# Two-layer block on one core: 169 low parts of weights made by ScalarE and an adding DMA instead of GpSimd

## The chip, the cores and the metric

The kernel runs on one core of one Trainium2 chip. A core has a matrix engine (PE), whose weight loads are listed as PEld, a vector engine (DVE), a scalar engine (ACT), a general engine (POOL, also GpSimd) and an engine that issues DMAs (SP). Each has its own instruction queue and works through it in order; they meet through semaphores. All DMAs share 16 DMA engines. Time is device microseconds of one execution, and the time of a kernel is the median of its runs.

## What is computed

The reference runs 512 tokens of width 1024 through two blocks. The first has two layers: a pooling and latent attention layer, then a differential attention layer, each followed by a gated feed-forward net. The second mixes three kinds of attention or recurrence and then routes each token to 128 of 16384 experts. What the change touches are the weights of the differential attention, of the second feed-forward net, of the mixing layer and of the router's queries:

```python
qkv = hn @ w_qkv                                   # differential attention
...
h = h + swiglu(rmsnorm(h, ffn_norm_g[layer]), ffn_w_gate[layer], ffn_w_up[layer], ffn_w_down[layer])
...
proj = h @ w_in[l]                                 # second block: 13 x 256 columns
...
x = x + mixed @ w_out[l]
...
q = (x_blk @ w_query).reshape(b, t, PEER_HEADS, 2, HALF_KEY)
scores = jnp.einsum('bthcd,hcnd->bthcn', q, sub_keys).astype(jnp.float32)
top_s, top_i = lax.top_k(scores, PEER_TOPK)
```

## The kernel before

Every large product is made of three products of a shorter float format: a weight w is split into a high part `whi` (w rounded) and a low part `wlo` = w - `whi`, the tokens likewise, and PE adds high by high, high by low and low by high (L266 to L268; L283 to L285 where tokens are rows). The function `load_w` brings a block of weights in two halves of up to 128x1024 float32 (512 KB). For a half SP issues a DMA into `raw` (L253), ACT copies `raw` into `whi` (L228), and DVE or POOL subtracts: `wlo` = `raw` - `whi` (L229, in `split`). `raw`, `whi` and `wlo` have three buffers each (`RB, WB = 3, 3`), shared by all weights in turn, so that a half can be begun only when PE has done with the half three before it. With 256 columns of tokens a half feeds 24 matrix products.

Who subtracts is set by `low(n)`: of the two halves of a block the first n go to POOL and the others to DVE. It is 2 in the differential attention (`LO_Q`), in the stage of memory and projections (`LO_Y`) and in the mixing and first routing stages (`LO_M`), 1 from the end of the first routing through the second half's projections (`LO_Z`) and in the last stages (`LO_P`), and 0 in the feed-forward nets ahead of the second block.

The stages follow each other in time roughly so, in us: differential attention 590 to 880; feed-forward of the first 256 tokens to 1070; memory and projections of half A 1075 to 1200; mixing of half A to 1322, its output, norm and first query blocks to 1422, the first routing to 1640; projections of half B to 1700, its mixing and output to 1850; then the expert stages to the end. The feed-forward of the other 256 tokens (`ffn_b`) is dealt out among the stages from 1075 to 1640 by `alongside`. Routing takes, for 8 heads and 2 tiles of tokens, the 16 largest of 128 scores twice and of their 256 sums once, all on DVE in some forty short instructions for each (L1465 to L1498).

A scheduler lays out each engine's queue from the program's order and priorities; the order is fixed when the kernel is built. In the expert stages POOL also issues gathers of 128 rows of 4 KB (L1503).

## Time and profile before

| | us |
|---|---|
| median of 3 runs | 3133.07 (3132.15 to 3140.36) |
| the profiled execution | 3134.13 |
| its span, first to last instruction | 3132.4 |
| PE busy | 2938.3 |
| DVE busy | 2207.6 |
| ACT busy | 1372.6 |
| POOL busy | 1147.2, of it subtractions of weights (L229, 241 of them) 589.8 |

Busy time is when an engine executes; waits and the issue of DMAs on SP are not in it. PE's clock has two levels, 1.2 and 2.4 GHz; the column "PEclk" or "clock" gives the granted share of the higher one. A wait is listed with the instruction that released it. The page cuts the span in 40 slices of 78.3 us; the views used below cut it at the stages' bounds.

### The profile page before, as it was taken

What the parts mean: (1) busy time and instruction counts of PE and PEld (TensorE: products, weight loads), DVE (VectorE), ACT (ScalarE), POOL (GpSimd) and SP (SyncE); (2) the same over time, 40 slices, a digit from 0 to 9 for tenths busy, and PEclk for the clock granted to TensorE, in tenths of its full rate; (3) what the DMA queues carried; (4) which work ended last, traced back from release to release, by engine and by line L of the source; (5) the groups of instructions that cost most, each with busy time, mean ns of one, the idle gap of its engine ahead of it and who ended that gap; (6) DMA issues with size and microseconds to landing.
All of it is one profiled execution on the core that took longest, in us unless ns stands there. A gap on an engine that the chain in (4) does not pass through costs nothing.

```text
span 3132.4 us, 44864 instructions
## 1 busy us (share of the span) xinstructions
PE 2938.3 (94%) x16770; PEld 2551.2 (81%) x16770; DVE 2207.6 (70%) x4148; ACT 1372.6 (44%) x2347; POOL 1147.2 (37%) x723
## 2 busy tenths in 40 slices
PE   8999999999989889998779989889999999999999
PEld 6468888867689888888769588888999998777787
DVE  6755434477766747658996569999787758888753
ACT  4443222466554545453244543336666653333333
POOL 3110000343320376466554235555554535445200
PEclk9999999999999989999889989999999999999999
DMA  3022232311145533234334038777788779999964
GB/s 132 25 67 101 88 101 88 107 54 48 35 158 194 175 132 125 87 132 142 118 112 151 1 121 281 254 274 256 275 316 305 283 286 383 382 380 370 338 229 151
DMA packets 195883, 568.30 MB, mean 181 GB/s; under 512 B 16944, under 2 KB 68528, under 8 KB 194000
## 3 DMA queue, kind: packets, MB, share of 16 engines
q1 hardware_dynamic: 157664, 427.61, 39.4%
q0 software_dynamic: 37712, 137.71, 11.9%
q8 instruction: 132, 2.16, 0.3%
q14 instruction: 87, 0.71, 0.1%
q10 hardware_dynamic: 288, 0.11, 0.0%
HBM read 512.93 MB, written 52.43 MB: 180 GB/s over the span
## 4 chain that ended last, share of the span: by engine, by line
PE 71%; DVE 21%; DMA 3%; issue 2%; ACT 2%; POOL 0%; DVEq 0%; SPq 0%; ACTq 0%; POOLq 0%
PE ps L266 15%; PE ps L267 15%; PE ps L268 15%; PE ps L1669 4%; PE ps L1670 4%; PE ps L1668 4%; PE ps L1550 2%; DVE u L1517 2%; DVE wlo L229 2%; PE ps L482 2%; DMA raw<-in_peer_v_dram 1%; PE ps L475 1%; DVE oh L1490 1%; PE ps L283 1%; PE ps L285 1%
## 5 line engine op out<-in xcount | busy, mean ns | idle before, releaser
L229 POOL TENSOR_TENSOR wlo<-raw,whi 128x1024 fp32r<-128x1024 f32 (+2 forms) x241 | 589.8, 2455 | 634.8 <-ACT whi L228 585.9
L228 ACT ACTIVATE whi<-raw 128x1024 fp32r<-128x1024 f32 (+2 forms) x518 | 516.2, 999 | 648.6 <-PE ps L267 391.8
L229 DVE TENSOR_TENSOR wlo<-raw,whi 128x1024 fp32r<-128x1024 f32 (+3 forms) x277 | 334.0, 1207 | 215.3 <-ACT whi L228 214.6
L268 PE MATMUL ps<-yh,wlo 128*128 128x384 f32 (+1 forms) x1152 | 387.5, 337 | 27.7 <-DVE wlo L229 27.6
L266 PE MATMUL ps<-yh,whi 128*128 128x384 f32 (+1 forms) x1152 | 389.9, 339 | 0.0
L267 PE MATMUL ps<-yl,whi 128*128 128x384 f32 (+1 forms) x1152 | 385.1, 334 | 0.0
L1669 PE MATMUL ps<-vl,gh 128*128 128x512 f32 x768 | 301.1, 392 | 4.2 <-DVE vl L229 4.1
L1670 PE MATMUL ps<-vh,gl 128*128 128x512 f32 x768 | 299.9, 391 | 0.0
L266 PE MATMUL ps<-XH,whi 128*128 128x512 f32 (+1 forms) x680 | 273.2, 406 | 8.7 <-ACT whi L228 8.7
L1503 POOL DMA_INDIRECT u<-in_peer_v_dram,ix x128 | 197.5, 1543 | 197.8 <-DVE h L1582 182.5
L267 PE MATMUL ps<-XL,whi 128*128 128x512 f32 (+1 forms) x680 | 267.7, 396 | 0.0
L268 PE MATMUL ps<-XH,wlo 128*128 128x512 f32 (+1 forms) x680 | 263.1, 395 | 1.3 <-DVE wlo L229 1.3
L1668 PE MATMUL ps<-vh,gh 128*128 128x512 f32 x768 | 239.8, 392 | 9.2 <-ACT vh L228 9.2
L268 PEld LDWEIGHTS ps<-yh,wlo 128*128 128x128 f32 x1152 | 220.4, 191 | 32.4 <-DVE wlo L229 32.4
L228 ACT ACTIVATE vh<-raw 128x1024 fp32r<-128x1024 f32 x128 | 133.5, 1056 | 253.9 <-DMA raw<-in_peer_v_dram 183.4
L266 PE MATMUL ps<-fx,whi 128*128 128x256 f32 x704 | 202.6, 292 | 26.0 <-ACT whi L228 21.4
L1517 DVE SCALAR_TENSOR_TENSOR u<-u,h 128x1024 f32<-128x1024 f32 x127 | 203.1, 1604 | 32.4 <-DMA u<-in_peer_u_dram,ix 32.2
L266 PEld LDWEIGHTS ps<-yh,whi 128*128 128x128 f32 x1152 | 220.9, 192 | 0.0
L267 PEld LDWEIGHTS ps<-yl,whi 128*128 128x128 f32 x1152 | 220.5, 191 | 0.0
L366 POOL TENSOR_TENSOR sqa<-sqa,sq 128x512 f32<-128x512 f32 (+1 forms) x28 | 42.1, 1505 | 450.5 <-ACT sq L364 449.6
L229 DVE TENSOR_TENSOR vl<-raw,vh 128x1024 fp32r<-128x1024 f32 x128 | 155.5, 1221 | 65.7 <-ACT vh L228 65.0
L267 PE MATMUL ps<-fx,whi 128*128 128x256 f32 x704 | 199.6, 287 | 0.9 <-DVE fx L351 0.9
(427 smaller groups left out, 7244.4 us busy)
## 6 DMA issues: line engine op xcount, KB each, us to landing
raw<-in_uT_dram SPq DMA_DIRECT2D x128, 512.0 KB
raw<-in_peer_v_dram SPq DMA_DIRECT2D x128, 512.0 KB
raw<-in_w_gate_dram SPq DMA_DIRECT2D x66, 512.0 KB
raw<-in_w_up_dram SPq DMA_DIRECT2D x66, 512.0 KB
raw<-in_w_in_dram SPq DMA_DIRECT2D x52, 512.0 KB
Sd<-s SPq DMA_DIRECT2D x32, 768.0 KB
Gd<-st SPq DMA_DIRECT2D x12, 2048.0 KB
gt<-Gd SPq DMA_DIRECT2D x32, 768.0 KB
```

Source lines behind the costliest of these rows:

```text
L228: SC.activation(hi, src, AF.Copy)
L229: eng.tensor_sub(lo, src, hi.bitcast(F))
L266: PE.matmul(out, wh, xh, start=first, stop=False)
L267: PE.matmul(out, wh, xl, start=False, stop=False)
L268: PE.matmul(out, wl, xh, start=False, stop=last)
L482: PE.matmul(po[hd], vtile(hd, j), t[hd, j], start=j == 0, stop=j == nk - 1)
L1503: i = GP.indirect_dma_start(out=u, out_offset=None, in_=A[table], in_offset=bass.IndirectOffsetOnAxis(ap=self.idx[t, hd][:, j:j + 1], axis=0))
L1517: V.scalar_tensor_tensor(u, u, 1.0, self.h2[t], op0=OP.mult, op1=OP.mult, accum_out=self.sd[t][:, hd, j:j + 1])
L1550: PE.matmul(p[:, n * 128:(n + 1) * 128], q[:, n], e[:, n], start=True, stop=True)
L1668: PE.matmul(p, gh[:, e, ts], h[:, cs], start=False, stop=False, skip_group_check=True)
L1669: PE.matmul(p, gh[:, e, ts], l[:, cs], start=False, stop=False, skip_group_check=True)
L1670: PE.matmul(p, gl[:, e, ts], h[:, cs], start=False, stop=end, skip_group_check=True)
```

## The change

A third value, `ADDED`, can stand where an engine stood. Such a half is loaded and copied to `whi` as before; then ACT also writes `wlo` = -`whi`, and POOL issues a DMA that reads the weights from DRAM once more and adds them into `wlo`. `raw` is no longer needed once `whi` is written. `low` is given `ADDED` for the differential attention, the projections, the mixing with the first routing, and the stage after it; the last stages keep POOL's subtraction.

```diff
-        def low(n):
-
-            LO[:] = [GP] * n + [V] * (2 - n)
+        ADDED = object()
+
+        def low(n, other=GP):
+
+            LO[:] = [other] * n + [V] * (2 - n)
...
-                split(hi, lo, raw, eng[i])
+                if eng[i] is ADDED:
+                    SC.activation(hi, raw, AF.Copy)
+                    SC.activation(lo, hi.bitcast(F), AF.Copy, scale=-1.0)
+                    GP.dma_start(lo, ap[:, a * w:b * w], accum_op=OP.add)
+                else:
+                    split(hi, lo, raw, eng[i])
...
-            low(LO_Q)
+            low(LO_Q, ADDED)
...
-        low(LO_Y)
+        low(LO_Y, ADDED)
         alongside((chain(memory(), projections(HA)), 24), (ffn_b, F_1))
         open_mix()
-        low(LO_M)
+        low(LO_M, ADDED)
...
-        low(LO_Z)
+        low(LO_Z, ADDED)
```

Of POOL's 241 subtractions of weights 72 stay; 169 become additions by DMA: 22 of `w_qkv`, 12 of `w_dout`, 4 of `w_mem`, 39 of `w_in`, 12 of `w_out`, 64 of the feed-forward net and 16 of `w_query`. ACT has 169 instructions more. Line numbers behind L262 grow by 7 (L266 becomes L273).

On ACT, in the projections of half A, before (`pj` and `hgv` are results of the projections, `sq` a gate):

```order
L228 ACTIVATE whi_9978<-raw_9976 128x1024
L1113 ACTIVATE hgv_9325<-ps_9918,rt_6972 128x256
L1113 ACTIVATE hgv_9325<-ps_9944,rt_6972 128x256
L228 ACTIVATE whi_10036<-raw_10034 128x1024
L228 ACTIVATE whi_10042<-raw_10040 128x1024
L1135 ACTIVATE sq_10516<-pj_9333 128x256
L228 ACTIVATE whi_10100<-raw_10098 128x1024
```

and the same blocks now:

```order
L259 ACTIVATE whi_10027<-raw_10025 128x1024
L260 ACTIVATE wlo_10028<-whi_10027 128x1024
L1120 ACTIVATE hgv_9359<-ps_9966,rt_7006 128x256
L1120 ACTIVATE hgv_9359<-ps_9992,rt_7006 128x256
L259 ACTIVATE whi_10086<-raw_10084 128x1024
L260 ACTIVATE wlo_10087<-whi_10086 128x1024
L259 ACTIVATE whi_10093<-raw_10091 128x1024
L260 ACTIVATE wlo_10094<-whi_10093 128x1024
L1142 ACTIVATE sq_10580<-pj_9367 128x256
L259 ACTIVATE whi_10152<-raw_10150 128x1024
```

Each copy is followed by the negated copy of the same half, and the other work has kept its place.

On POOL, in the first routing, before (the weights of `w_query` and `ffn_b` in turn):

```order
L229 TENSOR_TENSOR wlo_13767<-raw_13764,whi_13766 128x1024
L229 TENSOR_TENSOR wlo_13773<-raw_13770,whi_13772 128x1024
L229 TENSOR_TENSOR wlo_13855<-raw_13852,whi_13854 128x1024
L229 TENSOR_TENSOR wlo_13861<-raw_13858,whi_13860 128x1024
L229 TENSOR_TENSOR wlo_13987<-raw_13984,whi_13986 128x1024
```

and now:

```order
L261 DMA wlo_13667<-in_w_query_dram 128x1024
L261 DMA wlo_13674<-in_w_query_dram 128x1024
L261 DMA wlo_13757<-in_w_down11_dram 128x1024
L261 DMA wlo_13764<-in_w_down11_dram 128x1024
L261 DMA wlo_13891<-in_w_query_dram 128x1024
```

One DMA issue stands where one subtraction stood, and nothing else is between them in either.

On PE, in the projections of half A, where the second half of a block begins (`wlo_10043`, then `wlo_10028`), before:

```order
L266 MATMUL ps_10072<-xh_9293,whi_10042 128x256
L267 MATMUL ps_10072<-xl_9294,whi_10042 128x256
L266 MATMUL ps_10110<-xh_9293,whi_10100 128x256
L267 MATMUL ps_10110<-xl_9294,whi_10100 128x256
L266 MATMUL ps_10136<-xh_9293,whi_10100 128x256
L268 MATMUL ps_10046<-xh_9293,wlo_10043 128x256
```

and now:

```order
L273 MATMUL ps_10058<-xh_9327,whi_10027 128x256
L274 MATMUL ps_10058<-xl_9328,whi_10027 128x256
L273 MATMUL ps_10098<-xh_9327,whi_10086 128x256
L274 MATMUL ps_10098<-xl_9328,whi_10086 128x256
L273 MATMUL ps_10124<-xh_9327,whi_10086 128x256
L274 MATMUL ps_10124<-xl_9328,whi_10086 128x256
L275 MATMUL ps_10032<-xh_9327,wlo_10028 128x256
```

One product with a high part more runs ahead of the first with the low part (six instead of five); the order is otherwise as it was.

## Rows read from the trace of the kernel before

**Rows 1.** the page: the span, and busy time of each engine.

```profile
span 3132.4 us, 44864 instructions
PE 2938.3 (94%) x16770; PEld 2551.2 (81%) x16770; DVE 2207.6 (70%) x4148; ACT 1372.6 (44%) x2347; POOL 1147.2 (37%) x723
```

**Rows 2.** busy time by stage: from:to, length, PE, PEld, DVE, ACT, POOL, clock, DMA.

```profile
590.00:880.00 290.00, 284.84 (x1387) 211.03 (x1386) 202.78 (x482) 159.79 (x304) 115.17 (x74) 1.00 0.19 61
1116.00:1200.00 84.00, 79.44 (x660) 79.06 (x659) 31.88 (x70) 38.48 (x48) 63.71 (x28) 0.96 0.47 162
1200.00:1322.00 122.00, 109.20 (x751) 95.19 (x750) 94.57 (x237) 59.23 (x105) 60.72 (x50) 0.93 0.25 88
1322.00:1422.00 100.00, 92.67 (x747) 88.62 (x747) 56.05 (x131) 51.26 (x86) 62.62 (x27) 0.95 0.40 135
1422.00:1575.00 153.00, 116.16 (x899) 112.92 (x897) 150.71 (x505) 47.19 (x74) 82.56 (x35) 0.90 0.37 124
1575.00:1640.00 65.00, 48.71 (x297) 44.83 (x298) 62.31 (x171) 27.09 (x48) 35.18 (x34) 0.80 0.34 110
1640.00:1700.00 60.00, 60.00 (x518) 60.00 (x517) 29.05 (x49) 31.00 (x41) 27.57 (x11) 1.00 0.54 185
```

**Rows 3.** three of these stages, line 229 alone: DVE, then POOL.

```profile
1116.00:1200.00 84.00, 0.00 (x0) 63.67 (x27) 0.96 0.47 162
...
1322.00:1422.00 100.00, 14.91 (x21) 62.37 (x26) 0.95 0.40 135
1422.00:1575.00 153.00, 3.67 (x4) 82.56 (x35) 0.90 0.37 124
```

**Rows 4.** ACT in order of time, 1141 to 1151: start, length, idle's releaser.

```profile
1141.96 1.06 ACT L228 ACTIVATE whi<-raw 128x1024 fp32r<-128x1024 f32 x1 [1.53 <-PE ps L267]
...
1150.58 1.06 ACT L228 ACTIVATE whi<-raw 128x1024 fp32r<-128x1024 f32 x1 [1.24 <-PE ps L267]
```

**Rows 5.** a 512 KB transfer that POOL issued, and the wait for it.

```profile
L1007 POOL DMA_DIRECT2D mraw<-in_masks_dram x1: 536/536/536, 868.5 to 868.5; - x1
...
  DMA mraw<-in_masks_dram: 4.3, 1
```

**Rows 6.** POOL's DMA queue; its gathers of 512 KB: last, median us to landing.

```profile
q0 software_dynamic: 37712, 137.71, 11.9%
...
u<-in_peer_v_dram,ix POOLq DMA_INDIRECT x128, 7.8
u<-in_peer_u_dram,ix POOLq DMA_INDIRECT x127, 6.3
...
q<-in_peer_u_dram,ix POOLq DMA_INDIRECT x1, 4.6
```

**Rows 7.** groups of DVE, 1422 to 1575: count, busy us, mean ns.

```profile
L1488 DVE CAST af<-ai 128x16 f32<-128x16 int32 x24 | 20.1, 869 | 0.0
L1477 DVE TENSOR_TENSOR cand<-ts 128x256 f32<-128x256 f32 x13 | 13.9, 1071 | 0.0
L1485 DVE TENSOR_SCALAR ai<-bp 128x16 int32<-128x16 int32 x24 | 11.3, 508 | 0.0
...
L1492 DVE TENSOR_TENSOR oh<-oh,tf 128x256 f32<-128x256 f32 x23 | 9.7, 440 | 0.0
...
L1475 DVE CAST tf<-ti 128x32 f32<-128x32 uint32 x13 | 5.5, 423 | 0.0
```

**Rows 8.** groups of DVE and of POOL, 1880 to 2050.

```profile
L1488 DVE CAST af<-ai 128x16 f32<-128x16 int32 x20 | 2.9, 221 | 0.0
...
L1503 POOL DMA_INDIRECT u<-in_peer_u_dram,ix x40 | 50.2, 1254 | 24.7 <-DVE u L1517 5.7 <-DVE sc L1467 3.9 <-DVE ti L1466 3.6
```

**Rows 9.** DVE, then POOL, in order of time around 1494.

```profile
1494.03 2.23 DVE L1488 CAST af<-ai 128x16 f32<-128x16 int32 x2
...
1493.75 2.40 POOL L229 TENSOR_TENSOR wlo<-raw,whi 128x1024 fp32r<-128x1024 f32 x1 [0.98 <-ACT whi L228]
```

**Rows 10.** waits, 1422 to 1575: who, for whom, us in total, times, longest.

```profile
ACT sc L1459 <- DVE ti L1469: 30.4, 6, 14.7
```

## The prediction

> **What bounds the kernel now.** I read the page's busy times first, then the same by stage, then line 229 alone in three stages, then the instructions in order of time at two places. PE is busy 2938.3 of 3132.4 us [rows 1], so a change on other engines can win only where PE idles. By stage [rows 2] there are three kinds of stretch. In 590-880, 1116-1200 and 1640-1700 PE is busy 284.84 of 290, 79.44 of 84 and 60.00 of 60 us: PE is the bound. In 1422-1640, the first routing, DVE is: 150.71 of 153 and 62.31 of 65 us, with PE at 116.16 and 48.71. In 1200-1322 (mixing) and 1322-1422 no engine is full; PE leads with 109.20 of 122 and 92.67 of 100. Outside 590-1850 the change touches nothing.
>
> In the routing POOL holds DVE up. At 1494.03 two copies of 16 columns take 2.23 us; a subtraction of POOL runs from 1493.75 for 2.40, and they end together [rows 9]. The copy `af` costs 869 ns on average there and 221 in the second routing, where POOL subtracts less often and issues gathers [rows 7, 8]. The Trainium skill, "SBUF — State Buffer", section "Who interferes with whom", says why: DVE and GpSimd share one pair of ports as an exclusive lock. The trace agrees.
>
> **What goes.** 169 subtractions of 2.40 us leave POOL. On POOL they are covered everywhere, so that alone is worth nothing. What counts is DVE's blocked time in the routing: 24 x (869-221) ns = 15.6 us on `af`, 13 x (1071-440) = 8.2 on `cand` (against `oh`, of the same size), 24 x (508-221) = 6.9 on `ai`, 13 x (423-221) = 2.6 on `tf` [rows 7, 8]: 33 us at least of 1422-1575, nearly 1 us for each of its 35 subtractions [rows 3]. DVE's work there falls to about 117 us, level with PE's 116.
>
> **What comes.** ACT writes 169 more tiles at 1.06 us each for a full one [rows 4]. It is busy 38 of 84 us where PE is dense and 47 of 153 in the routing [rows 2]; it has room, and the time counts only as latency. POOL's issue takes 0.54 us [rows 5], less than the 2.40 it replaces, so what is queued behind it on POOL gains.
>
> The price is the time until the low part is there. Before, it is ready 2.40 us after `whi`. Now it takes the second ACT pass, 1.06, and a DMA. No accumulating DMA is in this trace. The nearest row is a plain transfer of the same 512 KB that POOL issued: issue 0.54, then POOL waits 4.3 for its landing [rows 5], about 4.9 in all. From below: a gather of 512 KB landed in 4.6, from above 7.8 under the load of the last stages [rows 6]. An addition must read its destination too; POOL's queue moved 137.71 MB in 11.9% of 16 engines' span [rows 1, 6], which is 1.4 us for 0.52 MB on 16 engines, and a second reading costs up to as much: 4.6 to 9.2, with 6.3 from the nearest row. I take 6.5, because the dense stretches already keep the DMA engines 0.47 busy [rows 2].
>
> The Trainium skill, "DMA: Bandwidth & Descriptors", section "Anatomy of one DMA — SWDGE (gpsimd) path", gives 2.0 us + bytes / 436e3 for a POOL-issued DMA. That is 3.2 us here, and the row says 4.9. By the page the landing would be 4.6 with a second reading, and the sum that of the first rival. The measured row decides.
>
> **Why latency reaches PE.** Only three buffers turn. PE's last product of a half releases its buffers; ACT can then begin the half three on; meanwhile PE has two halves left. In 1640-1700 PE makes 518 products in 60.00 us, 0.116 each [rows 2]; a half is 24 of them, 2.78 us. Before, one turn of a buffer is seen on ACT: the copy at 1141.96 and the one that follows it by three at 1150.58, 8.62 us [rows 4], little over three times 2.78. Low parts fit in that turn: 1.06 + 2.40 against 5.6 us of PE work in hand. Now a turn is 0.05 + 1.06 + 0.05 + 1.06 + 0.05 + 6.5 = 8.8 until the low part is there, plus 2.78 for the half itself, less 0.35 (six products with high parts that the order lets run ahead of every second half). That is 11.2 us for three halves, **3.73 us a half**, and PE waits for the difference.
>
> **The sum**, by stage:
> - 1116-1200: 27 halves [rows 3] in 84 us, 3.11 each; at 3.73: +17.
> - 1322-1422: 26 halves [rows 3]. The loop needs 97 us; PE's work on them is 26 x 2.78 = 72 of its 92.67, and the other 20 can lie beside the waits only in part. Half of the 25 that the loop lacks: +13.
> - 1075-1116: its halves partly wait for the norm anyway: +3.
> - 590-880: 34 halves in 290 us, 8.5 each, well over 3.73, so most is hidden. The last `w_dout` halves are half as large and follow closely: +5.
> - 1640-1700: every other half stays with DVE. Two turns are 11.2 + 4.8 for six halves, 2.67 each, below 2.78: hidden but for jitter, +2. The output of half B likewise, +2.
> - 1422-1575: 35 halves x 3.73 = 131 us is the new floor, above DVE's 117 and PE's 116. The three do not pack perfectly: ACT's copies stand in line behind steps that wait for DVE (`sc` waits 30.4 us for `ti` [rows 10]). I take 139 of 153: -14.
> - 1575-1640: half as many of POOL's subtractions, and DVE full: -4.
> - 1200-1322: DVE 94.57 of 122, 20-odd subtractions gone; PE has 13 us of idle time. A quarter of some 19 us of relief: -5.
>
> +42 - 23 = **+19**. Against the profiled execution, 3134.1, that is 3153; the median of the runs is 1 us lower: **3152**. For each us of landing, 60 dense halves / 3 give 20 us and 35 routing halves / 3 some 12: 32 us per us. The balance turns at a landing of 5.9.
>
> **Rivals.**
> 1. Faster. The addition lands as soon as the plain transfer, 4.9 us: the turn is 9.6, 3.20 a half. The dense stretches lose 8 in all, and the routing's floor is 112, so that DVE and PE (117) set it; at 122 it wins 31, with 9 more as above. -32: 3101. It decides below 5.9 us. For it: the DMA engines are half idle in all these stages [rows 2]. Against it: the second reading.
> 2. Much slower. The load of the late gathers (7.8) or a slow adder: at 8 us, 4.2 a half, +30 and +24 in the two dense stretches, +20 in the others, the routing back at 150: +66, 3199. At 9.2 about 3250.
> 3. Both effects cancel: a landing of 5.6 to 6.2, or the routing packs 15 us better. 3124 to 3142.
> 4. The issue itself is starved. In 1880-2050 POOL issues 40 gathers at 1254 ns each beside a full DVE [rows 8], so an issue there is at most 0.7 us longer than the 0.54 of the plain one [rows 5]. As a mechanism it would make each issue wait out DVE's copies, some 2 us on the landing: +80, 3215. The Trainium skill, "SBUF — State Buffer", section "SBUF: two separate sides", states it as a trap: DVE's two-port operations keep GpSimd from writing descriptors, 620 ns becoming 3100.
>
> That the change does not do what it says can be left out: the order on POOL shows a DMA for each subtraction.
>
> **How the numbers follow.** My forecast (slower by 9 to 50 us, 3143 to 3182) gets 0.34, rival 1 0.27, rival 2 0.18, rival 3 0.16, rival 4 0.05. A run tells 0.3%, 9.4 us, from no change: slower 0.57, same 0.16, faster 0.27. The range goes from rival 1 with its relief taken in full (routing at 117, mixing and the rest doubled: 3085) to a landing of about 8.4 (3215).
>
> **What would show it.** Right: in 1116-1200 the copies on ACT stand 11 us apart by threes, PE waits there for a DMA into `wlo`, that stage and 1322-1422 are 10 to 20 us longer, `af` costs under 250 ns in the first routing, and the routing is some 15 us shorter. The landing of the additions, issue to use, near 6.5 us. Wrong: a landing under 5.9, or a routing shorter by 30; or PE's clock, which is granted at 0.90 where PE idles a quarter and 1.00 where it is full [rows 2], falls in the dense stretches too and makes the loss larger than the waits.

## The result, and the profile after

The changed kernel takes **3256.7 us** (median; 3250.5 to 3265.7) where the kernel before takes 3136.7 (3132.2 to 3140.8) beside it: a ratio of 1.0385, 95% interval 1.0354 to 1.0416. The forecast was 3152, with 3215 as the upper end: the sign was right, the size was missed by a factor of six. (TensorE is PE, VectorE is DVE, ScalarE is ACT and GpSimd is POOL; a half is one 512 KB half of a block of weights.)

The profiled execution took 3250.5 us. Its page, answering [rows 1] and the queue line of [rows 6]: span, busy time of each engine, and of POOL's queue packets, MB and share of 16 engines.

```profile
span 3248.8 us, 45188 instructions
PE 2977.0 (92%) x16770; PEld 2579.7 (79%) x16770; DVE 2052.8 (63%) x4148; ACT 1531.3 (47%) x2516; POOL 900.6 (28%) x723
q0 software_dynamic: 62048, 222.66, 26.3%
```

Read span and PE together. The number of products is the same, 16770, but they kept TensorE busy 2977.0 us for 2938.3, and the rest of the span, idle time, is 271.8 us for 194.1. So the 116.4 us that the span grew are **77.7 us of more idle time and 38.7 us of slower products**. The second part is the clock: counted in the two traces, products that follow one of the same shape at about twice the spacing of the upper clock level cost 78 us more than at that level before, and 116 us now.

The stages, answering [rows 2]: from:to, length, PE, PEld, DVE, ACT, POOL, clock, DMA share, GB/s. The first three are the projections of half A, then the stretch up to the routing, the routing (two rows), and the feed-forward remainder with the projections of half B (two rows).

```profile
1110.00:1150.00 40.00, 32.97 (x225) 32.00 (x226) 6.84 (x25) 20.77 (x23) 9.86 (x19) 0.83 0.93 221
1150.00:1200.00 50.00, 35.37 (x242) 33.88 (x242) 6.49 (x22) 25.74 (x31) 9.20 (x11) 0.86 0.90 209
1200.00:1236.00 36.00, 27.77 (x194) 27.14 (x192) 6.80 (x28) 15.96 (x17) 6.04 (x7) 0.81 0.90 217
1343.00:1426.00 83.00, 68.15 (x470) 59.52 (x469) 34.88 (x125) 47.87 (x79) 14.16 (x19) 0.94 0.77 177
1490.00:1640.00 150.00, 113.20 (x844) 108.29 (x844) 103.71 (x518) 80.01 (x106) 28.54 (x33) 0.92 0.97 235
1640.00:1684.00 44.00, 30.41 (x225) 28.63 (x225) 31.33 (x134) 22.11 (x34) 6.65 (x8) 0.92 0.78 179
1684.00:1750.00 66.00, 48.86 (x338) 47.03 (x339) 22.48 (x46) 33.33 (x49) 20.30 (x33) 0.86 0.75 197
1750.00:1806.00 56.00, 44.67 (x334) 43.88 (x334) 17.29 (x39) 26.52 (x32) 5.20 (x6) 0.89 0.72 177
```

Three things stand here. TensorE idles 18 to 29% of the dense stages (all rows but the two of the routing), in which it idled 8% at most before. The DMA share of the projections went from 0.47 to 0.90 and more. And the clock, 0.95 to 1.00 in the dense stages before, is 0.81 to 0.94. A half is 24 products, so 661 products in the 126 us of the first three rows are 4.6 us a half, where 3.73 was forecast and 3.11 was before.

What TensorE waits for, 1074 to 1850 (who, for whom, us in total, times, longest):

```profile
PE ps L275 <- DMA wlo<-in_w_in_dram: 42.6, 17, 4.7
PE ps L275 <- DMA wlo<-in_w_down_dram: 23.8, 11, 3.8
PE ps L275 <- DMA wlo<-in_w_up_dram: 23.6, 14, 4.3
PE ps L275 <- DMA wlo<-in_w_query_dram: 18.2, 12, 2.6
```

The waits are for the adding DMAs, nearly all of them. Their landing after the issue (median us), and POOL's issue:

```profile
wlo<-in_w_in_dram POOLq DMA_DIRECT2D x39, 512.0 KB, 7.9
...
1721.28 0.86 POOL L261 DMA_DIRECT2D wlo<-in_w_in_dram  x1 [10.15 <-ACT wlo L260]
```

The plain 512 KB of [rows 5] had an issue of 0.54 us and landed in about 4.9; the adding one takes 0.86 and 7.9.

Where the 116 us arose, from marks that both traces have (us after the start before; then the difference of the changed kernel and of five experiments that are told below). A stick product is a product of queries and keys in the mixing's stick-breaking attention; the last step of the routing is its last reduction on DVE:

| mark | before | after | no DMA | plain DMA | every other | routing alone | last stage alone |
|---|---|---|---|---|---|---|---|
| first load of the memory's weights | 1072.7 | +1.2 | +3.0 | -5.6 | +2.4 | +6.3 | -0.5 |
| first stick product, half A | 1200.9 | +35.2 | -15.6 | +6.2 | +21.7 | +5.0 | -0.4 |
| last stick product, half A | 1298.6 | +44.9 | -34.9 | -0.9 | +15.2 | +4.5 | -0.3 |
| first MAX8 of the routing | 1424.3 | +66.0 | -38.1 | +2.4 | +30.9 | +1.8 | -0.3 |
| last step of that routing | 1634.1 | +49.9 | -105.5 | -45.4 | +7.4 | -13.1 | -10.6 |
| first stick product, half B | 1702.6 | +104.0 | -106.1 | -10.2 | +55.9 | +6.7 | +18.7 |
| first product of the experts' scores | 1851.5 | +108.4 | -112.1 | -8.0 | +71.7 | +3.4 | +24.1 |
| end | 3132.4 | +116.4 | -108.7 | -0.8 | +79.7 | +11.7 | +27.7 |

(Kernels that are alike up to a mark still differ there by up to 6 us, as the first line shows.) By stage the change cost 34 us in the memory and projections of half A (forecast 20), 10 in the mixing (forecast a gain of 5), 21 from there to the routing (forecast 13), gained 16 in the routing (forecast 18), and cost **54 between the routing and the mixing of half B (forecast 2)**.

### The profile page after: what moved, and what is told of

Its sections match the earlier page's. It is cut to its first block, busy times and chain, and to the rows that moved or that the text cites. A ratio compares the mean times of both kernels' runs of the same rounds, so it can differ in the third digit from the quotient of the medians.

```text
span 3248.8 us, 45188 instructions
## 1 busy us (share of the span) xinstructions
PE 2977.0 (92%) x16770; PEld 2579.7 (79%) x16770; DVE 2052.8 (63%) x4148; ACT 1531.3 (47%) x2516; POOL 900.6 (28%) x723
## 3 DMA queue, kind: packets, MB, share of 16 engines
q0 software_dynamic: 62048, 222.66, 26.3%
## 4 chain that ended last, share of the span: by engine, by line
PE 61%; DMA 13%; DVE 11%; issue 9%; ACT 3%; POOL 2%; POOLq 0%; SPq 0%; ACTq 0%; DVEq 0%
PE ps L275 13%; PE ps L273 13%; PE ps L274 13%; PE ps L1676 3%; PE ps L1677 3%; PE ps L1675 3%; PE ps L1557 3%; DMA wlo<-in_w_in_dram 2%; DMA raw<-in_peer_v_dram 2%; DVE wlo L229 2%; DVE u L1524 2%; PE ps L489 2%; DMA wlo<-in_w_up_dram 2%; DMA wlo<-in_w_query_dram 1%; DMA u<-in_peer_v_dram,ix 1%
## 5 line engine op out<-in xcount | busy, mean ns | idle before, releaser
L228 ACT ACTIVATE whi<-raw 128x1024 fp32r<-128x1024 f32 (+2 forms) x349 | 344.2, 987 | 517.4 <-PE ps L274 341.2
L273 PE MATMUL ps<-yh,whi 128*128 128x384 f32 (+1 forms) x1152 | 391.3, 340 | 0.0
L259 ACT ACTIVATE whi<-raw 128x1024 fp32r<-128x1024 f32 (+2 forms) x169 | 172.3, 1020 | 234.9 <-PE ps L274 212.4
L273 PE MATMUL ps<-XH,whi 128*128 128x512 f32 (+1 forms) x680 | 273.6, 406 | 8.7 <-ACT whi L228 8.7
L229 POOL TENSOR_TENSOR wlo<-raw,whi 128x1024 fp32r<-128x1024 f32 x72 | 199.5, 2771 | 295.1 <-ACT whi L228 279.2
L228 ACT ACTIVATE vh<-raw 128x1024 fp32r<-128x1024 f32 x128 | 133.7, 1055 | 260.5 <-DMA raw<-in_peer_v_dram 178.7
L275 PE MATMUL ps<-xh,wlo 128*128 128x256 f32 x576 | 172.1, 312 | 72.8 <-DMA wlo<-in_w_in_dram 42.6
L275 PE MATMUL ps<-fx,wlo 128*128 128x256 f32 x704 | 199.0, 292 | 38.3 <-DMA wlo<-in_w_up_dram 23.6
L273 PEld LDWEIGHTS ps<-yh,whi 128*128 128x128 f32 x1152 | 222.0, 193 | 0.0
L1524 DVE SCALAR_TENSOR_TENSOR u<-u,h 128x1024 f32<-128x1024 f32 x127 | 189.8, 1499 | 34.8 <-DMA u<-in_peer_u_dram,ix 34.7
L273 PE MATMUL ps<-fx,whi 128*128 128x256 f32 x704 | 200.2, 288 | 4.1 <-ACT fx L357 4.1
```

Of the source, the lines that this page charges most:

```text
L228: SC.activation(hi, src, AF.Copy)
L229: eng.tensor_sub(lo, src, hi.bitcast(F))
L259: SC.activation(hi, raw, AF.Copy)
L273: PE.matmul(out, wh, xh, start=first, stop=False)
L275: PE.matmul(out, wl, xh, start=False, stop=last)
L1524: V.scalar_tensor_tensor(u, u, 1.0, self.h2[t], op0=OP.mult, op1=OP.mult, accum_out=self.sd[t][:, hd, j:j + 1])
```

## Experiments

Two theories stood at the start. **Latency**: three buffers for the split halves can't cover a low part that is ready some 10 us after its raw half. **Throughput**: the adding DMAs fill the DMA engines, and no buffer helps. A third question was what the two extra ScalarE passes cost by themselves, and a fourth where the routing's gain went.

### The changed kernel without its DMA

```diff
                     SC.activation(hi, raw, AF.Copy)
-                    SC.activation(lo, hi.bitcast(F), AF.Copy, scale=-1.0)
-                    GP.dma_start(lo, ap[:, a * w:b * w], accum_op=OP.add)
+                    SC.activation(lo, hi.bitcast(F), AF.Copy, scale=0.001)
```

> The changed kernel without its adding DMAs: the low part is ScalarE's second copy alone (scaled by 0.001), so the addition of the weights is left out. Theory (landing): the 8 us that the addition takes to land are the whole loss. Without them a low part is ready 1.1 us after the high part, earlier than the 2.4 us of before; the dense stages stand as before, the routing of half A keeps its gain of 16 us or more, so 3095 to 3120 (0.987 to 0.996). Rival 1 (second copy): ScalarE's extra copies stand in line ahead of evictions and of the next high parts; then a good part of the loss stays without any DMA: 3160 to 3230. Rival 2 (a knock-on of the order: what runs beside what is shifted): some 50 us stay between the routing and the mixing of half B.

Measured: 3016.9 us, ratio 0.9612 (0.9596 to 0.9628). Both rivals fall, and the theory undershot: the routing's gain is not 16 us but 67 (see the table), and the whole is 120 us faster than before. The page (span and engines), and the routing's window:

```profile
span 3023.7 us, 44775 instructions
PE 2906.6 (96%) x16770; PEld 2529.9 (84%) x16770; DVE 2050.0 (68%) x4148; ACT 1527.6 (51%) x2516; POOL 755.2 (25%) x554
...
1386.00:1529.00 143.00, 135.91 (x1145) 134.76 (x1144) 142.40 (x662) 110.02 (x157) 13.72 (x17) 0.99 0.53 175
```

Some 1145 products and the routing's steps on DVE, which took 210 us before (DVE busy 208.5), take 143 here, at a clock of 0.99. TensorE's idle time over the span is 117.1 us, for 194.1 before. So what leaves POOL is worth far more than the prediction gave it, and the landing costs twice what the result shows. Ahead of the routing, where DVE is not full, 41 us are gained as well (-38.1 from +3.0); what of that is DVE's relief and what the earlier low part is not separated.

### A plain DMA in the adding one's place

```diff
-                    GP.dma_start(lo, ap[:, a * w:b * w], accum_op=OP.add)
+                    GP.dma_start(lo, ap[:, a * w:b * w])
```

> The changed kernel with the DMA of each low part a plain one (it overwrites the tile with the weights; the negative high part is lost, so the subtraction is left out). Same bytes from DRAM, same place in the order, no second reading of the destination. Theory A (the adding itself is slow: 4096 B packets take twice as long and the issue 0.86 us for 0.54): the landing falls from about 7.9 to 4.9 us, a turn of three buffers from 12.5 to 9.6 us, and the time to 3095 to 3130, no slower than before. Theory B (any transfer from DRAM between the two copies costs this much, since POOL's queue and the shared DMA engines are slow under the load of the stage): landing 7 us or more, time 3210 to 3260.

Measured: 3133.1 us, ratio 0.9997 (0.9979 to 1.0015). Theory A is the nearer: no slower than before, though 3 us above its range, with a landing of 5.4 us for the 4.9 that it named. The landing of the same row as above, the issue (min/median/max ns), and POOL's queue on the page:

```profile
wlo<-in_w_in_dram POOLq DMA_DIRECT2D x39, 512.0 KB, 5.4
...
L261 POOL DMA_DIRECT2D wlo<-in_w_in_dram x6: 527/527/527, 1120.3 to 1143.6; - x6
...
q0 software_dynamic: 62048, 222.66, 20.6%
```

Same packets, same bytes, 20.6% of 16 engines' span where the adding kernel has 26.3%. Against the 11.9% of 3132.4 us in [rows 6], the 84.95 MB more took (0.206 x 3131.6 - 0.119 x 3132.4) x 16 = 4358 us of engine time here and (0.263 x 3248.8 - 0.119 x 3132.4) x 16 = 7707 with the addition: 51 and 91 us per MB. **The addition makes a packet 1.8 times as dear** in the time that its packets take, about what a second reading at the price of the first would make it; that it is the second reading is not shown.

The three medians split the result: leaving POOL's subtraction out, 3137 to 3017, is -120; bringing the weights in a second time by a plain DMA +116; adding them in the DMA +124. Their sum is the +120 of the change.

### ScalarE's second pass alone

```diff
-                    GP.dma_start(lo, ap[:, a * w:b * w], accum_op=OP.add)
+                    GP.tensor_sub(lo, raw, hi.bitcast(F))
```

> The second copy on ScalarE stays, but instead of the adding DMA GpSimd subtracts as before into the same tile. The result is the kernel's. Theory (landing): a turn is 0.05 + 1.06 + 0.05 + 1.06 + 2.40 + 2.78 - 0.35 = 7.0 us, under three times 2.78, so nothing is lost: 3130 to 3150 (0.998 to 1.004). Rival (second copy on ScalarE costs by itself): 3170 or more.

Measured: 3147.3 us, ratio 1.003 (1.0016 to 1.0044). As the theory says: the extra passes on ScalarE, and the later start of the subtraction that they bring here, cost some 10 us (5 to 14 by the interval). They are not the cause.

### The routing alone

```diff
-            low(LO_Q, ADDED)
+            low(LO_Q)
...
-        low(LO_Y, ADDED)
+        low(LO_Y)
...
-        low(LO_M, ADDED)
+        low(LO_M)
...
+        low(LO_M, ADDED)
         alongside((PA.queries(), 140), (ffn_b, F_4), (gather_a, L_4))
-        low(LO_Z, ADDED)
+        low(LO_Z)
```

> The adding DMA only for the queries' weights of the first routing stage; everywhere else GpSimd subtracts as before. Theory: the first routing is 15 to 20 us shorter, as in the changed kernel (153.0 to about 137); the feed-forward products that ran beside it now run a little later, which gives back up to 10: 3112 to 3127 (0.992 to 0.997). Rival (the gain is given back in full: the products that filled the routing's idle TensorE time come behind it): 3131 to 3140. Rival 2 (the routing's gain came with the products' delay in the stages before, and is no gain without it): 3130 to 3150.

Measured: 3148.8 us, ratio 1.0034 (1.0021 to 1.0047). The theory falls. The time lies in the second rival's range, but not its mechanism: the routing is 15 us shorter here without any delay before it. What the trace shows is the first rival (the gain is given back), and more than all of it is given back. Three windows, the routing (two rows) and then what lies between it and half B's mixing, and below them the same two stretches of the kernel before:

```profile
1426.00:1560.00 134.00, 100.21 (x765) 95.43 (x764) 96.03 (x483) 71.91 (x93) 25.63 (x30) 0.95 1.00 241
1560.00:1621.00 61.00, 47.57 (x348) 44.90 (x346) 48.94 (x173) 32.39 (x52) 20.15 (x16) 0.90 0.68 172
1621.00:1709.00 88.00, 81.99 (x663) 81.68 (x664) 44.97 (x81) 42.91 (x59) 46.22 (x35) 0.92 0.51 174
```

```profile
1424.00:1634.00 210.00, 156.87 (x1143) 149.75 (x1143) 208.54 (x661) 70.35 (x116) 112.80 (x57) 0.87 0.36 119
1634.00:1703.00 69.00, 69.00 (x579) 68.88 (x580) 36.38 (x70) 34.87 (x45) 32.31 (x22) 0.97 0.53 180
```

The routing is 15 us shorter and the stretch behind it 20 us longer. Count TensorE's idle time over both: 283 - 229.8 = 53 us here; before, 279 us from 1424 to 1703 with 156.87 and 69.00 busy, 53 as well. DVE was relieved, but TensorE waited for the DMAs instead, and the products that it did not do there came later: 663 between the two marks, 579 before. 64 of these 84 were moved by the order itself: counted in the traces, TensorE has 911 products from the routing's last score product to half B's first stick product here, 847 before. And the DMA engines are full: share 1.00.

### Six buffers in the projections of half A

```diff
+        RING = [(wp, "whi", "wlo", WB)] * WB
+        TURN = [0]
+        def more_buffers(pool, n):
+            RING[WB:] = [(pool, "xhi", "xlo", n)] * n
+            TURN[0] = 0
...
-                hi = wp.tile([128, 1024], FR, name="whi", bufs=WB)[:, :c]
-                lo = wp.tile([128, 1024], FR, name="wlo", bufs=WB)[:, :c]
+                pool, nh, nl, nb = RING[TURN[0] % len(RING)]
+                TURN[0] += 1
+                hi = pool.tile([128, 1024], FR, name=nh, bufs=nb)[:, :c]
+                lo = pool.tile([128, 1024], FR, name=nl, bufs=nb)[:, :c]
...
+            if h is HA:
+                more_buffers(more.enter_context(tc.tile_pool(name="wq", bufs=1)), 3)
...
+        more = ExitStack()
         low(LO_Y, ADDED)
         alongside((chain(memory(), projections(HA)), 24), (ffn_b, F_1))
+        more.close()
+        more_buffers(None, 0)
```

> The changed kernel with six buffers for the split halves in place of three, during the projections of half A alone. There a half takes 4.3 us, and a turn of three buffers about 12.5. Theory A (latency: three buffers can't cover a low part that is ready 10 us after the raw weights): with six the half falls to 2.8 to 3.1 us, the stage is 40 to 50 us shorter than in the changed kernel, about as without any DMA, and the time 3200 to 3215. Theory B (throughput: the 16 DMA engines are busy 0.90 to 0.93 in that stage; an adding half takes about 2.6 us of all of them and its raw half 1.4): a half still takes about 4 us with six buffers, the landing grows to 12 us or more, and the time is 3240 to 3256.

Measured: 3244.5 us, ratio 1.035 (1.0322 to 1.0379): in theory B's range. The stage's windows, and the landing of the halves that use the added buffers (`xlo`):

```profile
1110.00:1150.00 40.00, 32.39 (x249) 30.58 (x248) 6.35 (x23) 24.17 (x25) 9.48 (x11) 0.96 1.04 265
1150.00:1200.00 50.00, 40.01 (x318) 37.58 (x317) 5.84 (x21) 29.82 (x31) 11.71 (x14) 1.00 1.05 275
...
xlo<-in_w_in_dram POOLq DMA_DIRECT2D x12, 512.0 KB, 14.2
```

318 products in 50 us are 3.8 us a half, for 4.6 with three buffers and 3.1 before; the landing went to 14.2 us, and 265 to 275 GB/s is what comes through at a share above 1. So both theories have a part: of the 1.5 us that a half lost in this stage, buffers return 0.8, and the DMA engines keep 0.7. Two times 0.524 MB at 272 GB/s are 3.9 us. Of the 19 us that the stage gained, 12 were lost again in the routing, where the clock was granted at 0.83 (1473 to 1678) for 0.92 in the changed kernel; why it was lower there stays open.

### The negative part first

```diff
-                    SC.activation(hi, raw, AF.Copy)
-                    SC.activation(lo, hi.bitcast(F), AF.Copy, scale=-1.0)
+                    SC.activation(lo, raw, AF.Copy, scale=-1.0)
                     GP.dma_start(lo, ap[:, a * w:b * w], accum_op=OP.add)
+                    SC.activation(hi, raw, AF.Copy)
```

> The changed kernel with another order of three instructions: ScalarE writes the negative rounded weights first, straight from the raw half, the adding DMA starts, and only then the high part is written. The result is the kernel's. The low part is ready about 1.1 us earlier against the raw half. Theory A (latency): 1.06 / 3 = 0.35 us less for each of some 120 halves that PE waits for: 3205 to 3225. Theory B (throughput of the DMA engines): the stages whose DMA share is over 0.9 don't move, those at 0.75 gain a little: 3240 to 3257. Rival C: the high part comes later, and PE's first products of a half wait for it: 3260 to 3290.

Measured: 3269.8 us, ratio 1.0437 (1.0414 to 1.0461). Theory A falls here. The time is rival C's, but its mechanism is not in the trace: TensorE's waits of line 273 for `whi` are 7.0 us, 6.3 in the changed kernel. Its waits for the adding DMAs grew, from 149 to 161 us by the rows of the waits view, and their landing from 7.9 to 8.4 for `w_in`. An earlier start bought nothing. That the DMA engines were full (a share of 0.90 and more in the projections of the changed kernel) would explain that much; why it cost 13 us is not settled.

### Every other half by DMA

```diff
             low(LO_Q, ADDED)
+            LO[1] = GP
...
         low(LO_Y, ADDED)
+        LO[1] = GP
...
         low(LO_M, ADDED)
+        LO[1] = GP
```

> The changed kernel, but where both halves of a weight went by the adding DMA only the first does; GpSimd subtracts the second as before. Half as many adding DMAs in the dense stages and the first routing. Theory A (latency): two turns hold three adding halves and three of 2.4 us: (12.5 + 8.6) / 6 = 3.5 us a half in the dense stages instead of 4.3; the routing keeps half of its relief: 3170 to 3200. Theory B (throughput): 1.4 + 2.6 / 2 = 2.7 us a half, under PE's 2.8, so the dense stages are nearly as before and the routing gains half of its relief: 3120 to 3145.

Measured: 3210.4 us, ratio 1.0238 (1.0212 to 1.0264). Slower than both theories allow. In the projections of half A:

```profile
1150.00:1222.00 72.00, 56.98 (x429) 55.38 (x428) 11.92 (x43) 32.23 (x38) 26.03 (x16) 0.91 0.72 175
```

4.0 us a half with the DMA engines at 0.72: not throughput, and not the 3.5 us that latency gave when two turns were averaged. The averaging is wrong, and it was the prediction's as well (below): the buffers turn by three, the kinds of half by two. A DMA half takes the buffer of the half three places earlier, which is a quick one (subtracted by POOL); it has to wait for that one's last product, then for its own landing, and TensorE takes the halves in order. From one quick half's end to the end of the quick half four places on there lie one latency and two halves of work: (10.5 + 2 x 2.8) / 4 = 4.0 us. This chain, the ring, was worked out after the run; the next two runs put it to the test.

### The last stage alone, with three buffers and with four

```diff
-            low(LO_Q, ADDED)
+            low(LO_Q)
...
-        low(LO_Y, ADDED)
+        low(LO_Y)
...
-        low(LO_M, ADDED)
+        low(LO_M)
```

> The adding DMA in the last of the four stages alone: the rest of the feed-forward products, projections, mixing and output of half B, where every other half stays with VectorE. Theory R (ring): a buffer comes back three halves on, so a DMA half waits for the buffer of a VectorE half, and four halves cost one latency and two halves of work: (10.5 + 2 x 2.8) / 4 = 4.0 us a half for some 24 halves that took 69 us before: +25 to +35 in that stretch, and 3160 to 3180 in all. Rival (averaging, as in the prediction: two turns with one latency each are shared by six halves, 2.7 us a half): 3135 to 3145. Rival 2 (what the changed kernel loses there comes from products that the shorter routing pushed back): 3137 to 3150.

Measured: 3166.1 us, ratio 1.0096 (1.0081 to 1.0112): in the ring's range and in neither rival's. From the last routing step to half B's first stick product the stretch is 29 us longer (table), and TensorE has 590 products in it for 571 before, so some 2 us of it are work that came later; up to 1424 nothing differs by more than 0.5. ScalarE and POOL in order of time (start, length; `L259` and `L228` are the copies of a DMA half and of DVE's half, `L260` the negative copy):

```profile
1644.19 1.06 ACT L259 ACTIVATE whi<-raw 128x1024 fp32r<-128x1024 f32 x1 [1.70 <-PE ps L274]
1645.77 1.04 ACT L260 ACTIVATE wlo<-whi 128x1024 fp32r<-128x1024 f32 x1
1647.11 0.86 POOL L261 DMA_DIRECT2D wlo<-in_w_in_dram  x1 [9.80 <-ACT wlo L260]
1649.38 1.06 ACT L228 ACTIVATE whi<-raw 128x1024 fp32r<-128x1024 f32 x1 [2.57 <-PE ps L274]
1650.74 1.06 ACT L259 ACTIVATE whi<-raw 128x1024 fp32r<-128x1024 f32 x1 [0.30 <-PE ps L274]
...
1658.70 1.06 ACT L228 ACTIVATE whi<-raw 128x1024 fp32r<-128x1024 f32 x1 [5.82 <-PE ps L292]
...
1661.86 1.05 ACT L259 ACTIVATE whi<-raw 128x1024 fp32r<-128x1024 f32 x1
```

The DMA half of 1644.19 and the one four places on, of 1661.86, are 17.7 us apart: 4.4 us a half (4.3 over the eight halves from 1644.19) for the chain's 4.0. DVE's half of 1649.38 is ready 2.3 us later and holds a buffer until 1658 without being used, and the DMA half of 1661.86 begins when TensorE has done with it.

The same with one buffer more in that stage:

```diff
         low(LO_Z, ADDED)
+        more = ExitStack()
+        more_buffers(more.enter_context(tc.tile_pool(name="wz", bufs=1)), 1)
...
         HB.output(MX["mix"])
         mixes.close()
+        more.close()
+        more_buffers(None, 0)
```

> As the run with the adding DMA in the last stage alone, with four buffers for the split halves there in place of three. Theory R (ring): a DMA half now takes the buffer of a DMA half, and four halves cost one latency and one half of work: (10.5 + 2.8) / 4 = 3.3 us a half: 15 to 20 us less than with three buffers. Rival (the DMA engines, busy 0.72 to 0.75 in that stage, set the time): within 6 us of the run with three.

Measured: 3169.6 us, ratio 1.0099 (1.0081 to 1.0117): the 15 to 20 us did not come. The time is the rival's, within 6 us of the run with three; its cause, the DMA engines, is not shown by a share of 0.78 for 0.70. The windows of both, three buffers first:

```profile
1640.00:1721.00 81.00, 64.19 (x484) 62.78 (x484) 23.60 (x50) 37.78 (x45) 7.76 (x9) 0.91 0.70 179
```

```profile
1640.00:1722.00 82.00, 66.08 (x510) 64.89 (x509) 26.59 (x61) 40.46 (x52) 8.62 (x10) 0.92 0.78 203
```

Its DMA halves start at 1641.1 and, eight halves on, at 1673.9: 4.1 us a half, not 3.3. The landing is the same, 7.4 us by the median in both. What is longer than reckoned is the time from the landing to the last product of the half, 4.0 to 5.6 us for 2.8: its products lie among those of the next half, and the first of them run at the lower clock. And the 8 us that the stretch gained from the routing's last step on were lost beside it: the routing took 7 us more than with three buffers (206.5 for 199.5), the mixing behind 4 (77 us from the first to the last stick product for 73). The share of each is not separated. So the traces show copies that wait for a buffer, and the chain foretold the time with three; that it is the whole price is not shown.

### The routing with seven buffers

The kernel with the DMA in the routing alone, and a pool of four more buffers there:

```diff
         low(LO_M, ADDED)
+        more_r = ExitStack()
+        more_buffers(more_r.enter_context(tc.tile_pool(name="wr", bufs=1)), 4)
         alongside((PA.queries(), 140), (ffn_b, F_4), (gather_a, L_4))
...
+        more_r.close()
+        more_buffers(None, 0)
         HB = Half(W, big)
```

> The adding DMA in the first routing stage alone (as in the earlier run, which took 3148.8), now with seven buffers for the split halves there. Theory A (latency): TensorE's waits for low parts in the routing fall away, and the relief of VectorE shows: 3095 to 3120. Theory B (throughput: the DMA share of that stage was 1.00 with three buffers): 3135 to 3150, as with three.

Measured: 3121.2 us, ratio 0.9954 (0.9942 to 0.9966), 28 us less than with three and 1 us above theory A's range. Here latency was most of it. And the control, the same lines in the kernel before (without `low(LO_M, ADDED)`):

> The kernel before, with seven buffers for the split halves in the first routing stage and no adding DMA anywhere: the control for the run with the adding DMA in that stage and seven buffers, which took 3121.2. If the seven buffers alone made the gain (TensorE runs ahead of the routing whatever makes the low parts): 3115 to 3127. If the relief of VectorE from GpSimd's subtractions made it (the routing is VectorE's, 208.5 of 210 us busy, and no buffer shortens that): 3132 to 3142, as before.

Measured: 3139.4 us, ratio 1.0002 (0.999 to 1.0014): the buffers alone do nothing, DVE is full:

```profile
1424.00:1640.00 216.00, 169.34 (x1256) 164.80 (x1255) 211.43 (x671) 74.18 (x123) 115.21 (x61) 0.87 0.36 121
```

The gain takes both: DVE's relief, and buffers enough that TensorE need not wait for the low parts.

With seven buffers the routing runs at a DMA share of 1.05 (below), so the next run halves the adding DMAs and gives the other halves to DVE:

```diff
-        low(LO_M, ADDED)
+        low(1, ADDED)
         more_r = ExitStack()
         more_buffers(more_r.enter_context(tc.tile_pool(name="wr", bufs=1)), 4)
         alongside((PA.queries(), 140), (ffn_b, F_4), (gather_a, L_4))
```

> The adding DMA in the first routing stage alone, with seven buffers, and there for the first half of each weight only; VectorE subtracts the second half, GpSimd none. With both halves by DMA that stretch moved 273 GB/s at a DMA share of 1.05. Theory B (there the DMA engines are the limit, VectorE had 27 us of 124 free): some 20 subtractions of 1.23 us are 25 us more on VectorE, the DMA's load falls by a third; VectorE and TensorE are then level near 115 to 125 of those 124: 3108 to 3122. Rival (VectorE is the limit again): 3122 to 3140.

Measured: **3116.2 us, ratio 0.9925 (0.9912 to 0.9937)**, 0.75% under the kernel before, and faster than both kernels. The first 124 us of the routing from its first MAX8 on, both halves by DMA (first) and the first half only:

```profile
1436.00:1560.00 124.00, 108.22 (x858) 105.69 (x856) 96.91 (x485) 74.69 (x100) 27.46 (x32) 0.94 1.05 273
```

```profile
1439.00:1563.00 124.00, 115.72 (x970) 114.62 (x968) 116.89 (x478) 64.55 (x94) 23.90 (x20) 0.99 0.86 228
```

A DMA share of 0.86 for 1.05, and TensorE is busy 93% of the stretch at a clock of 0.99, for 87% at 0.94.

## Why the prediction missed

**The landing** (the step "I take 6.5"). The bounds, 4.6 and 9.2, held for the medians (7.0 to 8.7 for the groups of 512 KB), while single landings took up to 11.6; the measured median of `w_in` is 7.9, and 8.6 among six issues in the projections. The 6.5 was 4.9 for the plain transfer [rows 5], 1.4 for the second reading and 0.2 for the load. Measured beside each other, the plain transfer takes 5.4 and the addition 2.5 more. For the hand-over of 0.05 us no row stands; in the rows of the last stage 0.3 us lie between the negative copy and POOL's issue. The rule of price was half right: the balance was put at a landing of 5.9 us, and the plain DMA breaks even at 5.4; above it each us costs 124 / 2.5 = 50 us, not 32.

**A limit that was not reckoned** (the dense stages: 34 us were lost for the +17 and +3, 21 for the +13). The copies on ACT stand 14 us apart by threes (1136.06 and 1150.26), for the 11 that the prediction named. The DMA engines' share of 0.47 in the dense stretches [rows 2] was used to lengthen the landing, and never as a load of its own. It says that a half's raw load takes 0.47 x 3.11 = 1.5 us of all engines; with POOL's 91 us per MB, which only the trace after shows, the low part adds 0.524 x 91 / 16 = 3.0. Even with twice that of the plain queue, 1.4 by the prediction's own working, the sum was 1.5 + 2.8 = 4.3 us against 2.78 of TensorE's work: the upper bound of the second reading made the DMA engines the bound, and this was there to be read. The six-buffer run shows it: 3.8 us a half at the share of 1.05.

**The ring** (the step on 1640-1700, "Two turns are 11.2 + 4.8 for six halves, 2.67 each, below 2.78: hidden but for jitter, +2"). Between the routing and half B's mixing lies the largest single miss, +54 for +2. The averaged 2.67 us a half failed: 4.0 were measured with every other half by DMA, 4.4 in the last stage alone. With the prediction's own landing the chain gives (8.8 + 2 x 2.8) / 4 = 3.6 us, above 2.78, some 20 us on 24 halves. The last stage alone shows +29, and the run with the routing alone +20, which the routing had pushed back: 49 of the 54. The sum is rough. Counted from the routing's first MAX8, so with what the routing gained, the two runs lose 19 and 5 us of the changed kernel's 38; the other 14 stay open, and so does why a fourth buffer did not help.

**The routing** (-14 and -4). Its length was forecast well, 193.7 us for 209.8, and by luck: DVE's relief was more than twice what was reckoned (below), and the waits for the low parts took the difference back. `af` fell as named, under 250 ns. DVE now waits: for ScalarE's scores 15.9 us, which was 2.8 before, and for TensorE's products some 46 us. The lines of DVE before (1424 to 1634), then after (1490 to 1684):

```profile
L1488 DVE CAST af<-ai 128x16 f32<-128x16 int32 x32 | 21.2, 699 | 0.0
...
L1465 DVE MAX8 ts<-sc 128x8 f32<-128x128 f32 x32 | 8.1, 283 | 2.8 <-ACT sc L1459 2.8
```

```profile
L1495 DVE CAST af<-ai 128x16 f32<-128x16 int32 x32 | 4.0, 179 | 0.0
...
L1472 DVE MAX8 ts<-sc 128x8 f32<-128x128 f32 x32 | 7.9, 282 | 15.9 <-ACT sc L1466 15.9
```

But a shorter stage is a gain only if TensorE's idle time falls with it, and that was not asked: TensorE had 60 us of 1640-1700 full [rows 2], so whatever it does not do in the routing lengthens that stretch. The relief itself was sized at 33 us "at least" from four groups [rows 7]; DVE's busy time in the routing fell by 208.5 - 103.7 - 31.3 = 73 us. The Trainium skill, "SBUF — State Buffer", section "Who interferes with whom", was the reason given, DVE and GpSimd as exclusive holders of one pair of ports, and the traces agree: 699 ns for `af` over the whole routing before, 179 here, with POOL's work there down from 112.8 to 35.2 us, while MAX8, with one input, kept its 283 and 282 ns. "On POOL they are covered everywhere, so that alone is worth nothing" did not hold ahead of the routing: without the DMA 41 us were gained there.

**The mixing** (-5). It cost 10. Its halves turn in the same three buffers; the loop was priced for its neighbours and left out there. With every other half on POOL it gained 6.5, without the DMA 19.

**The clock.** It stands in the prediction's last sentence as a way to be wrong, without a price. It is a third of the loss, 38.7 us. TensorE in the changed kernel, after one wait (start, length):

```profile
1729.06 0.58 PE L275 MATMUL ps<-xh,wlo 128*128 128x256 f32 x1 [3.43 <-DMA wlo<-in_w_in_dram]
1729.44 0.41 PE L273 MATMUL ps<-xh,whi 128*128 128x256 f32 x1
1729.65 0.41 PE L274 MATMUL ps<-xl,whi 128*128 128x256 f32 x1
...
1732.32 0.28 PE L275 MATMUL ps<-xh,wlo 128*128 128x256 f32 x1
1732.43 0.28 PE L273 MATMUL ps<-xh,whi 128*128 128x256 f32 x1
```

After 3.43 us of waiting the products start 0.21 us apart, the lower of the two clock levels, and from 1732.2 on 0.11 apart, the upper. The 14 products up to there took 3.1 us, 1.5 more than at full speed, on top of the wait. Not every wait does this. After another, of 3.12 us, the products start at the upper level:

```profile
1153.93 0.39 PE L291 MATMUL ps<-wlo,xh 128*128 128x256 f32 x1 [3.12 <-DMA wlo<-in_w_in_dram]
1154.15 0.28 PE L292 MATMUL ps<-whi,xl 128*128 128x256 f32 x1
1154.27 0.28 PE L290 MATMUL ps<-whi,xh 128*128 128x256 f32 x1
```

The waits view counts 74 waits for an adding DMA between 1074 and 1850; counted in the trace, 23 of them are followed at once by products at the lower level, 12 more within some thirty products, and 39 by none. In the dense stages before, the clock was 0.95 to 1.00 [rows 2]. The Trainium skill, "TensorE: Matmul & The Clock Gate", section "HAM oscillation — how this bites in real kernels", describes this pattern: products in short bursts with a DMA wait between them, and the clock dropping anew in each wait. The trace agrees in part, for about half of the waits.

**The rivals.** Rival 1 fell: a DMA that lands like a plain one (5.4 us) gives 3133, not 3101. Rival 2 had the right mechanism, and at a landing of 8 still only 3199, for the same missing terms (its +24 for 1322-1422 is +19 by the prediction's own halving: 26 x 4.24 = 110, less 72, halved). Rival 4, an issue that starves beside DVE's copies, is excluded: the 40 issues of the routing (1490 to 1684), where DVE is busy 104 of the first 150 us, took 863 to 889 ns. The attention stage (+5): the last raw half there is 5.6 us later, and the first load of the memory's weights 1.2; kernels that are alike up to there differ by up to 6 us, so this term is not tested. Of the stages behind 1851, which the change does not touch, 8 us stay unexplained.

## What to carry to other kernels

Moving work from an engine to a DMA is two prices, latency and load: for the first, follow the buffer's chain on the in-order engine that frees it, for the second, add up what all DMA engines have to do in that stage per unit of the busy engine's work. Count a gain on a side engine in the bound engine's idle time, not in the length of the stage; in one run here the routing grew 15 us shorter with the same 53 us of idle TensorE. And DMA waits that come back every few microseconds can cost clock as well as time, here half as much again as the added idle time.

## What the runs showed of the hardware

- An accumulating DMA of 512 KB from DRAM into SBUF: POOL's issue 0.86 us for 0.53 of the plain one, landing 7.9 us for 5.4, 91 us of engine time per MB for 51.
- With adding DMAs and plain loads in equal parts, no more than 265 to 275 GB/s came through (at a share of 1.04 to 1.05); without them the same page shows slices of 368 to 384 GB/s in the last stages.
- The Trainium skill, "DMA: Bandwidth & Descriptors", section "Anatomy of one DMA — SWDGE (gpsimd) path", gives 2.0 us + bytes / 436e3 for a DMA that POOL issues, an estimate of 3.2 us for the plain 512 KB. In the run with the plain DMA it took 4.9 to 6.4 by the medians of its groups, and the single transfer of [rows 5] took 3.6 to 5.8 in the traces of the other runs.
- One ScalarE pass more for 169 halves, with the later subtraction behind it, cost 0.16 to 0.44% of the time; leaving POOL's 169 subtractions out gained 3.9% beside that pass, over half of it in the routing, where DVE was held up.
